# Two-layer hybrid backbone: separate PSUM banks and a ScalarE bias for the modulation values, and the first queries on VectorE

## The chip, the cores and the metric

The kernel runs on one core of one Trainium2 chip. The metric is the device time of one execution in microseconds (us). Engines are named as in the profile: PE is TensorE with PEld its weight loads, DVE is VectorE, ACT is ScalarE, POOL is GpSimd, and SP is SyncE, which issues most of the DMA.

## The reference, cut to what matters

The model has two layers over 512 latent tokens and 256 context tokens of width 1024. Each layer takes six modulation vectors from a conditioning vector by one large product with `ada_w` and a bias; the first and the fourth shift, the second and the fifth scale as `1 + scale`, and the third and sixth weigh the residuals. Layer 0 mixes by a gated convolution of 31 taps beside an mLSTM, layer 1 by latent attention, and each layer ends in a feed-forward part with a short convolution.

```python
def _modulate(x, shift, scale):
    return _rms(x) * (1 + scale) + shift
...
def _conformer_mlstm_mixer(h_lat, h_ctx, w_in, gate_bias, conv_w, conv_b, ln_g, ln_b,
                           head_gain, w_out, with_ctx_out):
    lat = _ab_project(h_lat, w_in, gate_bias)      # a, g, q, k, v, o and the gates
    ctx = _ab_project(h_ctx, w_in, gate_bias)
...
        a, g, _, _, _, o, _, _ = p
        u = _dwconv(a * jax.nn.sigmoid(g), conv_w, conv_b)        # 31 taps
        u = jax.nn.silu(_layer_norm(u, ln_g, ln_b))
...
def _mla_mixer(...):
    def queries(cq, rotate):
        q = (_rms(cq) * q_norm) @ w_uq
        q = _rms(q.reshape(*q.shape[:2], MLA_HEADS, MLA_QK)) * q_gain
        return _rope_tail(q, cos, sin) if rotate else q
...
    for layer in range(DEPTH):
...
        mod_l = jnp.split((jax.nn.silu(c) @ ada_w[layer] + ada_b[layer])[:, None, :], 6, axis=-1)
        mod_c = jnp.split(jax.nn.silu(c_ctx) @ ada_w[layer] + ada_b[layer], 6, axis=-1)
        h_lat = _modulate(xl, mod_l[0], mod_l[1])
        h_ctx = _modulate(xc, mod_c[0], mod_c[1])
...
        xl = xl + mod_l[2] * y_lat
        xl = xl + mod_l[5] * _conv_ffn(_modulate(xl, mod_l[3], mod_l[4]), ffn_w_in[layer],
                                       ffn_conv_w[layer], ffn_conv_b[layer], ffn_w_out[layer])
```

## The kernel before

All work is written for one stream of tokens, 768 columns wide (512 latent, 256 context), with channels on the 128 partitions. Products in float32 are split in a high and a low part (`wh`, `wl` for weights, `hh`, `hl` for activations) and three products of these are summed, so each block of weights costs one ScalarE copy (`wh`), one subtraction on VectorE or POOL (`wl`) and three matmuls. Tiles, semaphores and the order on each engine come from the tile framework: each engine works through its own instructions in order, and a write to a buffer waits for the buffer's last readers.

**Modulation values of layer 0.** Each of the six vectors is made in two halves of 512 columns. A unit is one half of one vector: `pada` is the product of the conditioning vectors with a block of `ada_w` (16 matmuls, `ada_mm`), `arow` its copy to SBUF by ScalarE (`ada_rows`), `pac` the sum over the four row groups, transposed to columns by four matmuls (`ada_cols`), and `mods` the sum with the bias `adab` (`ada_bias`), on VectorE. For the vectors that scale, a second operation adds 1, by way of the tile `amod`. Vectors 1 and 0 come first (`ada_first`). The six units of vectors 2, 3 and 4 come from the generator `ada_pe`, which is advanced while the values V of the mLSTM are projected (`vproj`). Per step it loads a unit's weights (`wa`, two loads of 1 MB by SP), finishes the unit before the last (`pac`), and multiplies the last (`pada`). Vector 5, and all of layer 1, is summed on VectorE instead (`ada_gemv`, `ada_sum`).

**Stages of `mixer0`, in the order of PE.** The first conv tile (`pa` and `pg` are the two halves of the gated unit), the gates `pgt`, the second tile, the projections `pqk`, the third and fourth tile, V (`pv`, in four parts of weights), then the column sums `pcol`, the gate `po` and the mLSTM (`pu` to `pn`). Of each conv tile, ScalarE evacuates `up` and `sg`, VectorE multiplies them (`up<-sg,up`), ScalarE writes the first tap into `acc`, and VectorE adds the other 30 taps one by one (`acc<-up,par,acc`, 128x783). The taps are a background list from which each step of the projections takes a few; VectorE works on them long after PE has passed on.

**PSUM.** The eight banks are one pool per stage, by tags. Until the mLSTM, the pool `WIDE` has one tag S with four buffers of two banks each. `psum` takes from S; `psum1`, for results of one bank (`pada`, `pac`), takes from a tag T where there is one, and from S otherwise.

```python
    def psum1(self, s="ps"):
        return self.pt("T" if "T" in self.ptags else "S", s)
```

**Queries of layer 1.** `prep_q` projects four heads' queries (`puq`), scales them by the reciprocal root of their mean square (`rq`) and rotates them. The first group is called from `mixer1` with POOL as the engine for the scaling and the rotation (one operation of 128x1536 and eight smaller ones); the others are called from `attention`. PE then turns queries and keys (`ptr<-ident,qt`, `ptr<-ident,kt`) for the scores.

## Time and profile before

| | us |
|---|---|
| median of 3 runs (lowest, highest) | 1783.36 (1781.83, 1787.54) |
| the profiled execution | 1782.59 |
| its span, first to last instruction | 1780.8 |
| PE busy | 1679.1 (94%) |
| VectorE busy | 1130.3 (63%) |
| ScalarE busy | 679.2 (38%) |
| POOL busy | 246.0 (14%) |
| mean granted clock of TensorE, of 1 | 0.960 |

Times in the rows below are counted from the start of the span. A row of the timeline gives start, duration (of all its instructions where it stands for several), and in brackets how long the engine was idle before and what ended that. Matmuls of one accumulation overlap, so the distance between two starts is the better measure of what one costs.

### The profile page before, as it was taken

The numbers are of one execution on the slowest core, as the hardware profiler recorded it, in microseconds if no ns is written. First come the engines' busy times: TensorE is split into PE (matmuls) and PEld (weight loads), VectorE is DVE, ScalarE is ACT, GpSimd is POOL, SyncE is SP. The second block draws the span as 40 slices with busy tenths as digits, with TensorE's granted clock in tenths as the row PEclk, the third lists the DMA queues.
The fourth block names the chain that finished last, engine by engine and source line by source line (L and its number), as shares of the span: only waits on it lengthen the run. The fifth ranks groups of instructions, "written<-read, shape, count | busy, mean of one in ns | idle before, by whom it ended". The sixth has DMA issues, their size and how long they took to land.

```text
span 1780.8 us, 24171 instructions
## 1 busy us (share of the span) xinstructions
PE 1679.1 (94%) x9436; PEld 1519.1 (85%) x9436; DVE 1130.3 (63%) x1743; ACT 679.2 (38%) x1364; POOL 246.0 (14%) x331
## 2 busy tenths in 40 slices
PE   6998698769999999999999998999999799999999
PEld 3998476659899999999999878999988788888887
DVE  3799964745876555474334487777788854444544
ACT  4421042542331221212222346777876442332232
POOL 2342132425100000000000111223140200000000
PEclk8999799779999999999999999999999899999999
DMA  9621442233253345262221332001110133333332
GB/s 311 216 61 42 135 143 83 61 118 100 74 159 106 108 142 166 84 200 67 64 60 49 97 96 61 32 13 36 44 35 25 36 95 97 101 98 95 95 95 83
DMA packets 194747, 168.43 MB, mean 95 GB/s; under 512 B 8552, under 2 KB 168214, under 8 KB 194632
## 3 DMA queue, kind: packets, MB, share of 16 engines
q1 hardware_dynamic: 191936, 163.30, 29.8%
q0 software_dynamic: 1280, 3.35, 0.8%
q8 instruction: 75, 1.23, 0.3%
q10 hardware_dynamic: 1416, 0.21, 0.1%
q14 instruction: 40, 0.33, 0.1%
HBM read 161.55 MB, written 5.29 MB: 94 GB/s over the span
## 4 chain that ended last, share of the span: by engine, by line
PE 81%; DVE 10%; DMA 3%; ACT 3%; issue 1%; POOL 1%; SPq 0%; ACTq 0%; DVEq 0%; POOLq 0%
PE pfo L110 17%; PE pfg L110 16%; PE pfv L110 16%; DVE acc L593 6%; PE psc L110 4%; PE pab L110 3%; PE ppv L110 2%; PE pt L1409 2%; PE po L110 2%; PE pf L110 2%; PE pmo L110 2%; PE puq L110 2%; PE pukv L110 2%; PE pv L110 1%; PE pn L110 1%
## 5 line engine op out<-in xcount | busy, mean ns | idle before, releaser
L113 ACT ACTIVATE wh<-wr 128x1024 fp32r<-128x1024 f32 (+3 forms) x205 | 204.4, 999 | 625.0 <-PE pfo L110 215.5
L167 DVE TENSOR_TENSOR wl<-wr,wh 128x1024 fp32r<-128x1024 f32 (+3 forms) x171 | 195.8, 1147 | 194.4 <-ACT wh L113 190.5
L110 PE MATMUL pfo<-hh,wh 128*128 128x384 f32 (+2 forms) x528 | 166.8, 355 | 0.0
L110 PE MATMUL pfo<-hl,wh 128*128 128x384 f32 (+2 forms) x528 | 166.6, 355 | 0.0
L110 PE MATMUL pfo<-hh,wl 128*128 128x384 f32 (+2 forms) x528 | 166.2, 354 | 0.0
L110 PE MATMUL pfg<-fh,wh 128*128 128x384 f32 (+1 forms) x504 | 152.0, 355 | 0.0
L110 PE MATMUL pfg<-fl,wh 128*128 128x384 f32 (+1 forms) x504 | 151.6, 354 | 0.0
L110 PE MATMUL pfg<-fh,wl 128*128 128x384 f32 (+1 forms) x504 | 151.2, 354 | 0.0
L110 PE MATMUL pfv<-fh,wl 128*128 128x384 f32 (+1 forms) x504 | 150.8, 353 | 0.0
L110 PE MATMUL pfv<-fl,wh 128*128 128x384 f32 (+1 forms) x504 | 150.8, 353 | 0.0
L110 PE MATMUL pfv<-fh,wh 128*128 128x384 f32 (+1 forms) x504 | 150.7, 353 | 0.0
L119 DVE SCALAR_TENSOR_TENSOR xr<-pfo,mods,xr 128x512 f32<-128x512 f32 (+1 forms) x128 | 83.7, 665 | 104.4 <-PE pfo L110 103.8
L593 DVE SCALAR_TENSOR_TENSOR acc<-up,par,acc 128x783 f32<-128x783 f32 x120 | 146.9, 1249 | 4.4 <-ACT acc L113 2.3
L167 POOL TENSOR_TENSOR wl<-wr,wh 128x1024 fp32r<-128x1024 f32 (+1 forms) x34 | 85.3, 2512 | 296.9 <-ACT wh L113 280.2
L253 POOL TENSOR_TENSOR ss<-ss,sq 128x256 f32<-128x256 f32 (+1 forms) x31 | 32.1, 1044 | 573.5 <-ACT sq L113 572.6
L119 DVE SCALAR_TENSOR_TENSOR ga<-gr,cc,ga 128x1024 f32<-128x1024 f32 (+1 forms) x84 | 96.0, 1161 | 22.6 <-DMA gr<-in_ada_w_dram 22.3
L110 PEld LDWEIGHTS pfo<-hl,wh 128*128 128x128 f32 x528 | 98.1, 189 | 8.9 <-issue 0.2
L110 PEld LDWEIGHTS pfo<-hh,wh 128*128 128x128 f32 x528 | 97.9, 189 | 9.0 <-ACT hh L113 0.4
L110 PEld LDWEIGHTS pfo<-hh,wl 128*128 128x128 f32 x528 | 97.9, 189 | 8.7
L116 DVE TENSOR_TENSOR ft<-ft,pfv 128x768 f32<-128x768 f32 (+1 forms) x42 | 34.4, 820 | 109.9 <-PE pfv L110 109.9
L110 PEld LDWEIGHTS pfg<-fh,wh 128*128 128x128 f32 x504 | 92.8, 189 | 6.5
L110 PEld LDWEIGHTS pfg<-fl,wh 128*128 128x128 f32 x504 | 92.8, 189 | 6.4
(418 smaller groups left out, 3711.0 us busy)
## 6 DMA issues: line engine op xcount, KB each, us to landing
wr<-in_ffn_w_in_dram SPq DMA_DIRECT2D x88, 512.0 KB, 4.0
gr<-in_ada_w_dram SPq DMA_DIRECT2D x48, 512.0 KB, 4.5
wa<-in_ada_w_dram SPq DMA_DIRECT2D x20, 1024.0 KB, 8.1
wr<-in_ffn_w_out_dram SPq DMA_DIRECT2D x32, 512.0 KB, 3.5
wr<-in_ab_w_in_dram SPq DMA_DIRECT2D x20, 512.0 KB, 5.2
wr<-in_ffn_w_out_dram SPq DMA_DIRECT2D x24, 384.0 KB, 3.3
gr<-in_ada_w_dram SPq DMA_DIRECT2D x16, 256.0 KB, 2.7
wr<-in_mla_w_out_dram SPq DMA_DIRECT2D x8, 512.0 KB, 3.4
```

The lines of the kernel that those rows point to most:

```text
L110: self.nc.tensor.matmul(out, lhsT=lhsT, rhs=rhs, start=start, stop=stop)
L113: self.nc.scalar.activation(out, in_, func, **kw)
L116: self.nc.vector.tensor_tensor(out, a, b, op=op)
L119: self.nc.vector.scalar_tensor_tensor(out, a, s, b, op0=op0, op1=op1, **kw)
L167: self.lo_eng.tensor_tensor(lo[:, :n], raw[:, :n], hi[:, :n].bitcast(F32), op=ALU.subtract)
L253: eng.tensor_tensor(self.ss[:, s:e], self.ss[:, s:e], sq[:, s:e], op=ALU.add)
L593: nc.vector.scalar_tensor_tensor(acc[:, :CONVO], up[:, k:k + CONVO], self.convw[:, 4 * k + ct:4 * k + ct + 1], acc[:, :CONVO], op0=ALU.mul ...
L1409: nc.tensor.transpose(pt[:, o:o + P], pe[:, (j + jj) * P:(j + jj + 1) * P], self.ident)
```

## The change

Four edits. Until the mLSTM, the eight banks are three double banks (tag S) and two single ones (tag T, for `pada`, `pac` and the other results of one bank). For the six units of `ada_pe`, ScalarE adds the bias to `pac`, by one activation of 128x2 for each of the four columns of a half. The 1 of the scaling vectors is added to the bias itself, once per layer (`one_plus`). And the first group of queries is scaled and rotated by VectorE.

```diff
--- before.py
+++ after.py
@@ -69,6 +69,7 @@
 AFR = 4
 RUNS = (0, 0, 4, 4, 1, 1, 5, 5, 2, 2, 6, 3, 3, 7)
 WIDE = {"S": (2, 4)}
+FRONT = {"S": (2, 3), "T": (1, 2)}
 MLSTM = {"S": (2, 2), "M": (2, 2)}
 
 VW = P + 1
@@ -285,12 +286,12 @@
         self.act(rows, ps[:, :512])
         return rows
 
-    def ada_cols(self, rows, layer, mod, k1):
+    def ada_cols(self, rows, layer, mod, k1, on_act=True):
 
         p2 = self.psum1("pac")
         for k in range(4):
             self.mm(p2[:, 2 * k:2 * k + 2], rows[:, k * P:(k + 1) * P], self.selq, True, True)
-        self.ada_bias(p2, layer, mod, k1, 4)
+        self.ada_bias(p2, layer, mod, k1, 4, on_act)
 
     def ada_first(self, h, pool):
 
@@ -303,7 +304,7 @@
                 self.nc.sync.dma_start(raw, w[k * P:(k + 4) * P, c0:c0 + 512].rearrange("(k p) c -> p k c", p=P))
                 for kk in range(4):
                     self.ada_mm(ps, raw[:, kk], k + kk)
-            self.ada_cols(self.ada_rows(ps), 0, mod, 4 * h)
+            self.ada_cols(self.ada_rows(ps), 0, mod, 4 * h, False)
 
     def ada_pe(self, layer, mods, pool):
 
@@ -365,17 +366,21 @@
                 self.mm(p2[:, 2 * k:2 * k + 2], a[:, k * P:(k + 1) * P], self.selv[:, v, :], v == 0, v == len(accs) - 1)
         self.ada_bias(p2, layer, mod, k1, n)
 
-    def ada_bias(self, p2, layer, mod, k1, n):
+    def ada_bias(self, p2, layer, mod, k1, n, on_act=False):
         o = self.mods[layer][:, mod, k1:k1 + n, :]
         k0 = mod * KD + k1
-        b = self.adab[layer][:, k0:k0 + n].unsqueeze(2).to_broadcast([P, n, 2])
+        b = self.adab[layer][:, k0:k0 + n]
         pv = p2[:, :2 * n].rearrange("p (k v) -> p k v", v=2)
-        if mod in (1, 4):
-            tmp = self.small.tile([P, KD, 2], F32, tag="amod", name=self.name("amod"))[:, :n]
-            self.tt(tmp, pv, b, ALU.add)
-            self.nc.vector.tensor_scalar(o, tmp, 1.0, None, op0=ALU.add)
+        if on_act:
+            for k in range(n):
+                self.act(o[:, k], pv[:, k], AF.Identity, bias=b[:, k:k + 1])
         else:
-            self.tt(o, pv, b, ALU.add)
+            self.tt(o, pv, b.unsqueeze(2).to_broadcast([P, n, 2]), ALU.add)
+
+    def one_plus(self, ab):
+
+        x = ab[:, :48].rearrange("p (m k) -> p m k", k=KD)[:, 1::3]
+        self.nc.vector.tensor_scalar(x, x, 1.0, None, op0=ALU.add)
 
     def setup(self):
         nc, tc, d, ctx = self.nc, self.tc, self.d, self.ctx
@@ -430,6 +435,7 @@
         nc.vector.tensor_copy(self.cc32[:, :, :2], self.cc)
         ab = ctile([P, 48], "adab0")
         nc.vector.tensor_copy(ab, pa[:, 16:64])
+        self.one_plus(ab)
         self.adab.append(ab)
 
     def cols_load(self, q, st, parts):
@@ -481,6 +487,7 @@
         nc.vector.tensor_scalar(self.convw[:, :4 * CW], self.convw[:, :4 * CW], 0.5, None, op0=ALU.mult)
         nc.vector.tensor_scalar(v[:, 0:12], v[:, 0:12], 0.5, None, op0=ALU.mult)
         nc.vector.tensor_scalar(v2[:, 88:89], v2[:, 88:89], float(QK) ** -0.5, None, op0=ALU.mult)
+        self.one_plus(ab)
         self.adab.append(ab)
         self.lng, self.lnb, self.hgain, self.qnorm, self.kvnorm = (
             v[:, 0:4], v[:, 4:8], v[:, 8:12], v[:, 12:16], v[:, 16:18])
@@ -1225,7 +1232,7 @@
                     nc.vector.tensor_scalar(kvt[t][:, :256], kvt[t][:, :256], rk[:, t:t + 1], None, op0=ALU.mult)
                 qt0 = self.query_tile(ap)
                 for _ in self.prep_q(0, qt0, cqs, tb, wuq, lambda: tmp("sq")[:, :4 * QK].rearrange("p (h c) -> p h c", c=QK),
-                                     [xs[k][:, LAT:T] for k in (2, 3)], nc.gpsimd):
+                                     [xs[k][:, LAT:T] for k in (2, 3)], nc.vector):
                     pass
                 for k in range(2):
                     ps = self.psum("pkvT")
@@ -1530,7 +1537,7 @@
     def run(self):
         nc, tc = self.nc, self.tc
         pes = ExitStack()
-        self.psum_pool(pes, WIDE)
+        self.psum_pool(pes, FRONT)
         self.setup()
         xs = self.mixer0(pes)
         self.dump("x_mix0", xs)
```

Where the instructions move. On PE, in the V projection, the first `pac` (`pac_1520`, now `pac_1518`) was followed by nine matmuls of the second part of V and then by the second `pada`; these are the rows of the kernel before:

```order
L110 MATMUL pac_1520<-selq,arow_1463 128x2 x3
L110 MATMUL pv_165_1443<-wh_1538,hh_412 128x512
L110 MATMUL pv_165_1443<-wl_1539,hh_412 128x512 [waits Pool_49]
L110 MATMUL pv_165_1443<-wh_1538,hl_413 128x512
L110 MATMUL pv_165_1443<-wh_1538,hh_414 128x512
L110 MATMUL pv_165_1443<-wl_1539,hh_414 128x512
L110 MATMUL pv_165_1443<-wh_1538,hl_415 128x512
L110 MATMUL pv_165_1443<-wh_1538,hh_412 128x512
L110 MATMUL pv_165_1443<-wl_1539,hh_412 128x512
L110 MATMUL pv_165_1443<-wh_1538,hl_413 128x512
L110 MATMUL pada_1526<-wa_1450,cc_107 32x512 [waits DMAHW1_49,DVE_49]
L110 MATMUL pada_1526<-wa_1450,cc_107 32x512 x3
```

With the change the same place reads:

```order
L111 MATMUL pac_1518<-selq,arow_1461 128x2 [waits Activation_49]
L111 MATMUL pac_1518<-selq,arow_1461 128x2 x3
L111 MATMUL pada_1527<-wa_1448,cc_107 32x512 [waits DMAHW1_49,PE_49]
L111 MATMUL pada_1527<-wa_1448,cc_107 32x512 x3
L111 MATMUL pada_1527<-wa_1449,cc_107 32x512 [waits DMAHW2_49]
L111 MATMUL pada_1527<-wa_1449,cc_107 32x512 x3
L111 MATMUL pv_163_1441<-wh_1539,hh_409 128x512
L111 MATMUL pv_163_1441<-wl_1540,hh_409 128x512 [waits Pool_49]
```

The second `pada` has moved ahead of the second part of V, and its wait for VectorE (`DVE_49`) has become one for PE's own earlier use of the bank. The `pac` that follows comes behind all 36 matmuls of that part.

On ScalarE, from the `arow` of the first unit to that of the second, before (`acc_1426` is the first tap of the fourth conv tile):

```order
L113 ACTIVATE arow_1463<-pada_1454 128x512 [waits PE_49]
L113 ACTIVATE acc_1426<-up_1418,par 128x783 [waits DVE_49,Pool_49]
L113 ACTIVATE wh_1680<-wr_1679 128x1024 [waits DMAHW1_49,PE_49,Activation_49]
L113 ACTIVATE arow_1535<-pada_1526 128x512 [waits PE_49,Activation_49]
L113 ACTIVATE wh_1831<-wr_1830 128x1024 [waits DMAHW2_49,PE_49,Pool_49]
```

And with the change:

```order
L114 ACTIVATE arow_1461<-pada_1452 128x512 [waits PE_49]
L114 ACTIVATE acc_1424<-up_1416,par 128x783 [waits DVE_49,Pool_49]
L114 ACTIVATE wh_1687<-wr_1686 128x1024 [waits DMAHW1_49,PE_49,Activation_49]
L114 ACTIVATE mods_111<-pac_1518,adab_194 128x2 [waits PE_49]
L114 ACTIVATE mods_111<-pac_1518,adab_194 128x2 x3
L114 ACTIVATE arow_1536<-pada_1527 128x512 [waits PE_49,Activation_49]
L114 ACTIVATE wh_1843<-wr_1842 128x1024 [waits DMAHW2_49,PE_49,Pool_49]
```

Four additions of the bias (`mods`) have come in ahead of the second `arow`, and all of them stand behind `acc`, which waits for VectorE.

On VectorE, in the preparation of the attention, from the last step of `rq` on; `v` are evacuations of the values, `wl` low parts of weights, and what follows leads to the scale `rk` of the keys. Before:

```order
L119 SCALAR_TENSOR_TENSOR rz_8602<-rz_8602,ra_8601 128x16
L119 SCALAR_TENSOR_TENSOR rq_8600<-rz_8602,rq_8600 128x16
L116 TENSOR_TENSOR v_8675<-pukv_8677,v_8675 128x4x64
L167 TENSOR_TENSOR wl_8915<-wr_8913,wh_8914 128x768
L116 TENSOR_TENSOR v_8675<-pukv_8698,v_8675 128x4x64
L116 TENSOR_TENSOR ssk_8676<-ssk_8676,ssr 128x12
L199 TENSOR_SCALAR ra_8742<-ssk_8676 128x12
L116 TENSOR_TENSOR v_8675<-pukv_8719,v_8675 128x4x64
```

And with the change, up to the last but two of the nine operations that POOL had:

```order
L120 SCALAR_TENSOR_TENSOR rz_8610<-rz_8610,ra_8609 128x16
L120 SCALAR_TENSOR_TENSOR rq_8608<-rz_8610,rq_8608 128x16
L1308 TENSOR_TENSOR qt_8526<-qt_8526,rq_8608 128x1536
L117 TENSOR_TENSOR v_8683<-pukv_8685,v_8683 128x4x64
L1316 TENSOR_TENSOR xr_2911<-qt_8526,sq 128x128
L168 TENSOR_TENSOR wl_8923<-wr_8921,wh_8922 128x768
L1316 TENSOR_TENSOR xr_2911<-qt_8526,sq 128x128
L1316 TENSOR_TENSOR xr_2913<-qt_8526,sq 128x128
L1318 TENSOR_TENSOR qt_8526<-qt_8526,cq 128x8x32
L1316 TENSOR_TENSOR xr_2913<-qt_8526,sq 128x128
L1319 TENSOR_TENSOR qt_8526<-qt_8526,xr_2911 128x8x32
L1318 TENSOR_TENSOR qt_8526<-qt_8526,cq 128x8x32
```

The scaling of `qt` and the rotation (`xr`, `qt`) now stand between `rq` and the sums `ssk` of the keys; on POOL the same nine are gone.

## Rows read from the trace of the kernel before

**Rows 1.** The page, part 4: share of each engine in the chain.
```profile
PE 81%; DVE 10%; DMA 3%; ACT 3%; issue 1%; POOL 1%; SPq 0%; ACTq 0%; DVEq 0%; POOLq 0%
```

**Rows 2.** Windows: stretch, its length; busy us (instructions) by engine; granted clock; DMA share, GB/s.
```profile
180.00:230.00 50.00, 32.34 (x166) 21.56 (x165) 49.11 (x49) 5.65 (x7) 10.82 (x3) 0.83 0.46 149
```

**Rows 3.** Timeline of PE, 160 to 290 us: start, duration, instructions, [idle before <-releaser].
```profile
174.62 0.63 PE L110 MATMUL pv<-wl,hh 128*128 128x512 f32 x1
...
179.31 0.60 PE L110 MATMUL pv<-wh,hh 128*128 128x512 f32 x1
...
182.30 0.95 PE L110 MATMUL pac<-selq,arow 128*128 128x2 f32 x8
...
203.11 3.64 PE L110 MATMUL pada<-wa,cc 128*32 128x512 f32 x16 [17.66 <-DVE mods L116]
...
207.18 0.39 PE L110 MATMUL pv<-wl,hh 128*128 128x512 f32 x1
...
213.22 0.95 PE L110 MATMUL pac<-selq,arow 128*128 128x2 f32 x8
...
220.72 1.92 PE L110 MATMUL pada<-wa,cc 128*32 128x512 f32 x16
```

**Rows 4.** Timeline of DVE, 188 to 280 us.
```profile
191.24 0.69 DVE L119 SCALAR_TENSOR_TENSOR up<-sg,up 128x512 f32<-128x512 f32 x1
...
202.90 0.15 DVE L116 TENSOR_TENSOR mods<-pac,adab 128x8 f32<-128x8 f32 x1
...
276.06 0.42 DVE L116 TENSOR_TENSOR kw<-pu,wcol 128x256 f32<-128x256 f32 x1 [24.67 <-PE pu L958]
```

**Rows 5.** Timeline of ACT, 168 to 250 us.
```profile
174.81 0.81 ACT L113 ACTIVATE sg<-pg 128x768 f32<-128x768 f32 x1
...
193.30 1.04 ACT L113 ACTIVATE acc<-up,par 128x783 f32<-128x783 f32 x1 [17.19 <-DVE up L119]
194.25 1.04 ACT L113 ACTIVATE wh<-wr 128x1024 fp32r<-128x1024 f32 x1
206.88 0.60 ACT L113 ACTIVATE arow<-pada 128x512 f32<-128x512 f32 x1 [11.59 <-PE pada L110]
...
245.90 0.27 ACT L113 ACTIVATE ccol<-pcol 128x24 f32<-128x24 f32 x2 [1.82 <-PE pcol L881]
...
248.43 1.88 ACT L113 ACTIVATE ex<-ex,ccol 128x128 f32<-128x128 f32 x6
```

**Rows 6.** Timeline of PE, 219 to 262 us.
```profile
235.84 0.95 PE L110 MATMUL pac<-selq,arow 128*128 128x2 f32 x8
...
239.41 1.05 PE L110 MATMUL pac<-selq,arow 128*128 128x2 f32 x8 [0.78 <-ACT arow L113]
...
246.56 1.01 PE L110 MATMUL po<-hh,wh 128*128 128x384 f32 x2 [0.69 <-ACT em L113]
```

**Rows 7.** Timeline of PE, 17 to 50 us.
```profile
27.74 1.87 PE L110 MATMUL pac<-selq,arow 128*128 128x2 f32 x8 [0.78 <-ACT arow L113]
...
30.21 2.92 PE L110 MATMUL pb<-rx,runs 6*128 6x128 f32 x12 [0.37 <-DVE rx L560]
```

**Rows 8.** Timeline of POOL, 1095 to 1116 us.
```profile
1102.39 2.76 POOL L1301 TENSOR_TENSOR qt<-qt,rq 128x1536 f32<-128x1536 f32 x1 [65.86 <-DVE rq L119]
```

**Rows 9.** Timeline of DVE, 1095 to 1116 us.
```profile
1102.05 0.18 DVE L119 SCALAR_TENSOR_TENSOR rq<-rz,rq 128x16 f32<-128x16 f32 x1
...
1104.44 1.52 DVE L167 TENSOR_TENSOR wl<-wr,wh 128x768 fp32r<-128x768 f32 x1 [0.79 <-ACT wh L113]
...
1108.52 0.65 DVE L119 SCALAR_TENSOR_TENSOR rz<-rz,ra 128x12 f32<-128x12 f32 x1
...
1112.22 0.96 DVE L1362 TENSOR_TENSOR kt<-kt,rk 128x768 f32<-128x768 f32 x1
1113.09 0.55 DVE L1363 TENSOR_TENSOR kt<-krr,rk 128x384 f32<-128x384 f32 x1
```

**Rows 10.** The page, part 6: DMA issues, KB each, us to landing.
```profile
wa<-in_ada_w_dram SPq DMA_DIRECT2D x20, 1024.0 KB, 8.1
```

## The prediction

> **What bounds the kernel now.** I read the chain that ended last first: PE has 81% of it and VectorE 10% [rows 1], so a change is worth what it gives PE where PE stands still. The windows show where that is: from 180 to 230 us PE is busy 32.34 of 50 us at a granted clock of 0.83, while VectorE is busy 49.11 [rows 2]. The timeline of PE names the wait: at 203.11 the modulation product `pada` starts after 17.66 us of idle that VectorE's `mods` ended [rows 3]. The timeline of VectorE shows this releaser: an addition of 0.15 us at 202.90, in order behind the taps of the convolution [rows 4]. It waited only because `pada` needed the bank that this addition reads. The reader is to see that PE waits for a tiny instruction in a long queue, and that VectorE itself then has 24.67 us to spare before its first `kw` [rows 4]: its taps end at 276.06 - 24.67 = 251.4.
>
> **The change part by part.**
>
> *Banks and the bias on ScalarE.* `pada` no longer waits for VectorE, but ScalarE becomes the next in line. Behind the `arow` of the first unit, its queue holds `acc` of the fourth conv tile, which waits for VectorE's `up` until 193.30, then `wh` at 194.25 (ending about 195.3) [rows 5]; behind these stand the four new additions and the next `arow`. The new order lets PE run the first `pac`, the second `pada` and all 36 matmuls of the second part of V, and then the second `pac` waits for that `arow`. So the wait is not removed: it becomes later and shorter.
>
> How far PE gets: the first `pac` starts at 182.30 and a `pada` takes 1.9 [rows 3]. From the `pac` at 235.84 over a `pada` and a wait of 0.78 to the next `pac` it is 3.57 us [rows 6], so a `pac` takes 3.57 - 0.78 - 1.9 = 0.89. A matmul of V takes (213.22 - 207.18)/26 = 0.232 us, so 36 take 8.35. PE stops at 182.30 + 0.89 + 1.9 + 8.35 = 193.4.
>
> When it goes on: no row shows an addition of 128x2 with a bias held in a tile. Bounds: the two `ccol` of 128x24 without one take 0.27 together, so 0.19 and then about 0.09 a step, 0.46 for four; the six `ex` of 128x128, which have such a bias, take 1.88, 0.31 each, of which at least 0.1 is for the 126 columns more, leaving about 0.2, so at most 4 x 0.23 = 0.93 [rows 5]. I take 0.9, for `ex` shares the bias operand. With 0.6 for `arow` [rows 5], PE goes on at 195.3 + 0.9 + 0.6 = 196.8, after an idle of 3.4 us.
>
> A rule of the Trainium skill speaks against this part: "ScalarE: Activation LUTs", section "What ACT_TABLE_LOAD costs", says that an activation pays a fixed start, longer with a bias from a tile (about 280 ns, consecutive ones overlapping by 93 ns), so that one operation split into four pays it four times. By the page, an estimate, the four would take about 0.85 us, and the total would come out 0.1 us lower than by the row that I use; no row here shows the operation itself.
>
> Before, PE reached the second `pac` at 213.22 [rows 3]: 16.4 us later. But after an idle the clock is lower: in the matmuls of V from 174.62 on, which follow a wait, eleven took (179.31 - 174.62)/11 = 0.43 each instead of 0.23 [rows 3], 2.3 us in all with a twelfth. I charge the new idle with the same 2.3 (bounds 0 and 2.3), and save nothing for the old one, since what that cost lay ahead of 213.22.
>
> From there to `po` the new order has five `pac` (4.45), four `pada` (7.6), two parts of V with 36 matmuls each (16.7), the 18 transposes `pcol`, one wait of 0.78 for `arow`, and 0.95 for the last four additions, for which `po` waits. `pcol` follows from the old end: 239.41 + 0.89 + 1.9 + 0.78 + 0.89 = 243.87, and to 246.56, less the wait of 0.69, 2.0 us are left [rows 6]. Sum 32.5; before it was 246.56 - 213.22 = 33.3, with one wait of 0.78 more, which `pcol` now covers. So `po` starts at 196.8 + 32.5 + 2.3 = 231.6 instead of 246.56: **15.0 us gained**.
>
> Is it carried on? VectorE's taps end at 251.4 less some 1 to 2 us for the additions taken out; `kw` is now wanted at 276.06 - 15.0 = 261.1. Some ten us are left, so VectorE does not become the bound. The loads of the last units: a `wa` lands 8.1 us after its issue [rows 10]; the last pair takes the buffers of the fourth `pada`, which by the steps above ends about 213, so it lands at 221 and is wanted at 227. That covers 6 us of delay in SP's queue.
>
> *Three double banks instead of four.* PE now waits for evacuations that a fourth bank covered. The narrowest place is the fourth conv tile: its `sg` is evacuated by 174.81 + 0.81 = 175.6 and used by VectorE at 191.24 [rows 4, 5]: 15.6 us of cover. I take 0 (bounds 0 and 1).
>
> *The start.* With `pr` and `pb` no longer in line behind a `pac` at 27.74, which waited 0.78 for `arow` and takes 0.89 [rows 7], they come about 1.7 us before the old 30.21, and everything that follows from `pb` (normalised tiles, first weights, first taps) with them. Bounds 0 and 2; I take **1.5 us gained**, and since VectorE's taps, which begin from there, fill it (49.11 of 50 us in the window above), it moves ScalarE's `acc` at 193.30, and so all of the above, by the same amount.
>
> *Queries on VectorE.* POOL's nine operations go; the first took 2.76 us for 128x1536 [rows 8]. On VectorE: from 384 columns in 0.55 and 768 in 0.96 [rows 9], 1536 take 0.96 + 2 x 0.41 = 1.8; four of 128x128 at about 0.2 and four of 256 at 0.34: 3.9 us added between 1102.2 and `kt`. Against that, while POOL ran, a `wl` of 128x768 took 1.52 instead of 0.96 and a small operation 0.65 (1108.52) instead of 0.18 (1102.05) [rows 9]. Some eight small ones stand there; at half of the 0.47 of that row, for not all are as slow, they and the `wl` give back 2.4 us. VectorE also waited 0.79 for ScalarE in front of that `wl` [rows 9] and about as much once more ahead of it; the new operations fill these 1.6 us. A further 0.7 comes off the copies of `v` and the later `wl`. So 3.9 added stand against 4.7 given back: `kt`, which ends at 1113.09 + 0.55 = 1113.6 [rows 9], and PE's transposes behind it, come **0.8 us earlier**. Bounds: 2 gained, or 4 lost if nothing is hidden.
>
> *The added 1 folded into the bias*: two short VectorE operations in the set-up, of some 0.2 us like the small ones above. In the feed-forward part the additions taken out have PE-bound work around them. I take 0 for both.
>
> Sum: 1782.59 (the profiled execution: its span of 1780.8 and 1.8 around it; the median of the runs is 0.8 above) - 15.0 - 1.5 - 0.8 = 1765.3. **I predict 1765 us.**
>
> **The rivals.**
>
> *A. The wait disappears altogether.* If `acc` comes as PE ends the part, neither the 3.4 us of idle nor the 2.3 of slow clock remain: 1765 - 5.7 = 1759. For it: nothing but that `up` could come earlier with the start. Against it: ScalarE works in order and `up` of the fourth tile depends on VectorE's taps, which moves by 1.5 only. 8%.
>
> *B. Part of it is handed back.* Each later `pac` waits a little longer for ScalarE, with its four additions ahead of the next `arow`, or the last `wa` pairs land late, and the clock stays low through the short waits: 3 to 8 us, so 1768 to 1773. For it: short waits of 0.78 and 0.69 are there already [rows 6]. Against it: in each of the two long parts 8 us of matmuls lie between a `pada` and its `pac`. 17%.
>
> *C. The change does not do what it says.* PE still waits for VectorE, only by way of ScalarE's `acc`, and the later gain is lost in the attention's preparation: with `po` at 240, the start at 0 and 4 lost behind `kt`, 1782.6 - 6.5 + 4 = 1780. For it: that chain of waits is real. Against it: `acc` comes at 193.30, ten us ahead of 202.90. 4%.
>
> *D. Slower.* With three double banks, PE in the gated unit waits for evacuations that stand in ScalarE's queue behind an `acc` waiting for VectorE, so `up` is late and the taps stop. The place is the fourth conv tile, ahead of 191.24. Up to 15.6 us it is covered; to pass the time before, the delay must reach 15.6 + 17.3 = 33 us. A hold of 40 us would give 1765 + 40 - 15.6 = 1789. For it: one bank less of four. Against it: the evacuations that free these banks stand ahead of the `acc` in ScalarE's order. 3%.
>
> **How the numbers follow.** My forecast has 68% and its own range is 1761 to 1768 (slow clock 0 to 2.3, start 0 to 2, additions 0.46 to 0.93, queries -2 to +4). With A below and most of B above, 1758 to 1771 leaves out less than 2 in 10. A difference under 0.3% (5 us) is about what this measurement can't tell from none. The forecast, A and B are faster: 93%; C and what else could cancel it give 4% within, D 3% slower.
>
> **What would show it right or wrong.** Right: the wait of `pada` for VectorE is gone; PE idles some 3 us before 196 (195 with the start's gain) and names ScalarE's `arow`; matmuls of V behind it take 0.43 for some five us; `po` starts near 230; VectorE waits for `pu` about 9 us instead of 24.67; in the attention's preparation no POOL work beside VectorE's, small VectorE operations of 0.17, `kt` a little sooner relative to `rq`. Wrong: a wait of PE for `wa` or `mods` between 200 and 230, a gap in the taps before 193, or a longer stretch from `rq` to `kt`.

## The result and the profile after

| | before | changed |
|---|---|---|
| median of the runs, us (lowest, highest) | 1785.45 (1781.83, 1788.24), 4 runs | 1767.49 (1762.60, 1771.46), 4 runs |
| ratio to before, 95% interval | | 0.9899 (0.9863 to 0.9936) |
| the profiled execution; its span, us | 1782.59; 1780.8 | 1762.60; 1760.4 |

The changed kernel is faster by 1.0%, some 18 us between the medians; 1765 was predicted. Its own executions differ among themselves: the two shorter ones have a mean granted clock of 0.966, the two longer ones 0.961 and 0.960; of the runs below, one of `change_wl`, of 2378 us at a granted clock of 0.646, is left out.

The timeline of PE in V, in the kernel after, answers to [rows 3]:
```profile
184.99 0.95 PE L111 MATMUL pac<-selq,arow 128*128 128x2 f32 x8
185.87 1.92 PE L111 MATMUL pada<-wa,cc 128*32 128x512 f32 x16
...
195.81 0.39 PE L111 MATMUL pv<-wh,hl 128*128 128x512 f32 x1
199.01 1.25 PE L111 MATMUL pac<-selq,arow 128*128 128x2 f32 x8 [2.81 <-ACT arow L114]
200.19 3.36 PE L111 MATMUL pada<-wa,cc 128*32 128x512 f32 x16
203.48 0.50 PE L111 MATMUL pv<-wh,hh 128*128 128x512 f32 x1
...
232.34 0.62 PE L111 MATMUL po<-hh,wh 128*128 128x384 f32 x2 [0.81 <-ACT mods L114]
```
The second `pada` follows its `pac` at once; the 17.66 us of idle in front of it are gone. In their place stand 2.81 us in front of the second `pac`, for ScalarE's `arow`. Behind it `pac` and `pada` run at a lower clock (3.36 instead of 1.92), and the matmuls of V from 203.48 are at full pace again. `po` comes at 232.34 instead of 246.56.

The windows of the kernel after (the stretch of [rows 2], then 11 us of which the last 1.8 are in the idle, and 4 us behind it; busy us of PE, PEld, DVE, ACT and POOL, granted clock, DMA share, GB/s):
```profile
180.00:230.00 50.00, 46.88 (x263) 32.51 (x262) 49.57 (x46) 14.81 (x48) 24.15 (x4) 0.94 0.62 209
...
187.00:198.00 11.00, 9.20 (x44) 6.68 (x36) 10.75 (x13) 2.12 (x4) 0.00 (x0) 1.00 0.70 235
199.00:203.00 4.00, 3.99 (x24) 1.75 (x24) 4.00 (x2) 1.62 (x5) 4.00 (x2) 0.59 0.18 40
```
PE now fills 46.88 of the 50 us instead of 32.34. The clock of 0.59 of its 2.4 GHz, nearly the level of 1.2 GHz, lies wholly behind the idle.

The timeline of ACT around the same place answers to [rows 5]:
```profile
195.88 1.04 ACT L114 ACTIVATE acc<-up,par 128x783 f32<-128x783 f32 x1 [17.20 <-DVE up L120]
196.83 1.04 ACT L114 ACTIVATE wh<-wr 128x1024 fp32r<-128x1024 f32 x1
197.78 0.69 ACT L114 ACTIVATE mods<-pac,adab 128x2 f32<-128x2 f32 x4
198.35 0.60 ACT L114 ACTIVATE arow<-pada 128x512 f32<-128x512 f32 x1
```
This is the chain that PE waits for, in ScalarE's order: `acc` waits 17.20 us for VectorE's `up`, and the four additions and `arow` stand behind it. The four take 0.69 us.

The timeline of DVE answers to [rows 4]:
```profile
193.82 0.69 DVE L120 SCALAR_TENSOR_TENSOR up<-sg,up 128x512 f32<-128x512 f32 x1
...
228.33 3.12 DVE L600 SCALAR_TENSOR_TENSOR acc<-up,par,acc 128x783 f32<-128x783 f32 x1
231.38 3.14 DVE L117 TENSOR_TENSOR s<-s,acc 128x783 f32<-128x783 f32 x1
...
255.61 0.97 DVE L117 TENSOR_TENSOR s<-s,acc 128x783 f32<-128x783 f32 x1
260.91 0.42 DVE L117 TENSOR_TENSOR kw<-pu,wcol 128x256 f32<-128x256 f32 x1 [4.33 <-PE pu L965]
```
The first `kw` is 15.15 us earlier (276.06 before), and VectorE has 4.33 us to spare in front of it instead of 24.67.

The timeline of PE at the start, from the profiled execution after, answers to [rows 7]:
```profile
20.21 1.92 PE L111 MATMUL pada<-wa,cc 128*32 128x512 f32 x16
...
25.48 2.80 PE L111 MATMUL pb<-rx,runs 6*128 6x128 f32 x12 [0.37 <-DVE rx L567]
...
30.92 1.87 PE L111 MATMUL pac<-selq,arow 128*128 128x2 f32 x8 [0.78 <-ACT arow L114]
32.72 3.47 PE L111 MATMUL pada<-wa,cc 128*32 128x512 f32 x16
38.99 1.61 PE L111 MATMUL pac<-selq,arow 128*128 128x2 f32 x8 [2.80 <-ACT arow L114]
...
44.95 1.87 PE L111 MATMUL pac<-selq,arow 128*128 128x2 f32 x8 [0.78 <-ACT arow L114]
46.68 0.99 PE L111 MATMUL pa<-hh,wh 128*128 128x384 f32 x2
```
`pb` is 4.7 us earlier, but the `pac` that was ahead of it is 3.2 later (30.92, before 27.74). The third `pada` is still a little earlier than before, and then PE waits longer for `arow`; the same two rows before:
```profile
33.07 3.54 PE L110 MATMUL pada<-wa,cc 128*32 128x512 f32 x16
...
37.40 1.05 PE L110 MATMUL pac<-selq,arow 128*128 128x2 f32 x8 [0.79 <-ACT arow L113]
```
The timeline of ACT in the kernel after shows where that `arow` stands:
```profile
37.73 0.72 ACT L114 ACTIVATE hh<-u,mods 128x512 fp32r<-128x512 f32 x1 [0.15 <-DVE u L120]
38.36 0.58 ACT L114 ACTIVATE arow<-pada 128x512 f32<-128x512 f32 x1
```

The timeline of DVE in the attention's preparation answers to [rows 9]:
```profile
1080.94 1.02 DVE L120 SCALAR_TENSOR_TENSOR kvl<-pkvT,par,kvh 128x768 fp32r<-128x768 f32 x1
...
1084.75 1.76 DVE L1308 TENSOR_TENSOR qt<-qt,rq 128x1536 f32<-128x1536 f32 x1
...
1086.96 0.96 DVE L168 TENSOR_TENSOR wl<-wr,wh 128x768 fp32r<-128x768 f32 x1
...
1091.26 0.17 DVE L120 SCALAR_TENSOR_TENSOR rz<-rz,ra 128x12 f32<-128x12 f32 x1
...
1093.59 0.96 DVE L1369 TENSOR_TENSOR kt<-kt,rk 128x768 f32<-128x768 f32 x1
```
The 128x1536 takes 1.76 on VectorE, where POOL took 2.76 [rows 8]; the `wl` takes 0.96 and the small operations 0.17, with no wait in front of the `wl`.

Where the 20.4 us between the two spans went: 15.15 are there at the first `kw`. From the first `kvl` to `kt` the changed kernel takes 12.65 instead of 13.78, and from `kt` to the first `psc` 3.08 instead of 3.67: 1.7 together. Most of the remaining 3.5 lies in stretches that the change does not touch: 2.1 from `kw` to the first feed-forward part, and 1.3 from `psc` to the second. The repeat below gives these back.

### The profile page after: what moved, and what is told of

Same layout as the page of the kernel before. It is cut to its first block, busy times and chain, and to the rows that moved or that the text cites. A ratio compares the mean times of both kernels' runs of the same rounds, so it can differ in the third digit from the quotient of the medians.

```text
span 1760.4 us, 24187 instructions
## 1 busy us (share of the span) xinstructions
PE 1674.3 (95%) x9436; PEld 1513.3 (86%) x9436; DVE 1133.5 (64%) x1742; ACT 683.6 (39%) x1388; POOL 254.7 (14%) x322
## 4 chain that ended last, share of the span: by engine, by line
PE 84%; DVE 10%; ACT 3%; issue 1%; DMA 1%; POOL 1%; SPq 0%; ACTq 0%; POOLq 0%; DVEq 0%
PE pfo L111 17%; PE pfg L111 17%; PE pfv L111 16%; DVE acc L600 4%; PE psc L111 4%; PE pab L111 4%; PE ppv L111 2%; PE pt L1416 2%; PE po L111 2%; PE pv L111 2%; PE pf L111 2%; PE pmo L111 2%; PE puq L111 2%; PE pukv L111 2%; PE pac L111 2%
## 5 line engine op out<-in xcount | busy, mean ns | idle before, releaser
L600 DVE SCALAR_TENSOR_TENSOR acc<-up,par,acc 128x783 f32<-128x783 f32 x120 | 151.2, 1285 | 4.5 <-ACT acc L114 2.3
L168 POOL TENSOR_TENSOR wl<-wr,wh 128x1024 fp32r<-128x1024 f32 (+1 forms) x34 | 100.9, 2975 | 265.5 <-ACT wh L114 248.8
```

Source lines behind the costliest of these rows:

```text
L168: self.lo_eng.tensor_tensor(lo[:, :n], raw[:, :n], hi[:, :n].bitcast(F32), op=ALU.subtract)
L600: nc.vector.scalar_tensor_tensor(acc[:, :CONVO], up[:, k:k + CONVO], self.convw[:, 4 * k + ct:4 * k + ct + 1], acc[:, :CONVO], op0=ALU.mul ...
```

## The experiments

Each kernel's runs alternated with runs of the kernel before on the same chip, whose median was 1784.4 to 1784.9; ratios are against it.

**The changed kernel once more**, without an edit.

> The changed kernel again, unaltered, so that the other runs have it on the same chip. Theory (the gain is PE's earlier return in the V projection, some 14 to 17 us, less about 2 lost at the start): the second pac starts near 199 after about 3 us of idle for ScalarE's arow, po starts at 232 +- 1, the median is 1762 to 1768. Rival (a part of the 20 us between the two profiled executions is a difference between executions): po near 232 all the same, but the median 1768 to 1772.

Measured: median 1769.95 (1763.74 to 1771.06, 5 runs), ratio 0.9911 (0.9896 to 0.9925). The profiled execution was one of the longer ones, at a granted clock of 0.960. PE waits 2.94 us for `arow` at 198.06, `po` comes at 234.74, `kw` at 263.89 behind 9.22 us of spare time. The two stretches that the change does not touch take 189.5 and 306.9 us, where before took 189.2 and 306.7 and the first profile 187.1 and 305.4. So the 3.4 us there are differences between executions. Together with the 4.33 and 9.22 us of slack, the reader sees how far one profile carries: some 3 us in a landmark, some 5 in a wait.

**The banks alone**: additions on VectorE as before, queries on POOL, the pool FRONT and the folded 1 kept.
```diff
-    def ada_cols(self, rows, layer, mod, k1, on_act=True):
+    def ada_cols(self, rows, layer, mod, k1, on_act=False):
...
-                                     [xs[k][:, LAT:T] for k in (2, 3)], nc.vector):
+                                     [xs[k][:, LAT:T] for k in (2, 3)], nc.gpsimd):
```

> Only the banks and the folded 1: the sums stay on VectorE, the first queries on POOL. Theory (banks and bias each free PE by half): the second pada starts at once, but the second pac reuses the bank of the first, which VectorE reads only behind its taps, so PE idles 7 to 9 us there, names DVE mods, goes on near 204.5, and po starts at 237 to 240; median some 6 us above the changed kernel. Rival (the banks alone do it): idle under 3.5 us, po within 1 us of the changed kernel, the time within 2 us of it.

Measured: 1782.74, ratio 0.9992 (0.9980 to 1.0004). The timeline of PE in this kernel:
```profile
206.21 1.84 PE L111 MATMUL pac<-selq,arow 128*128 128x2 f32 x8 [12.10 <-DVE mods L117]
...
240.81 1.84 PE L111 MATMUL pac<-selq,arow 128*128 128x2 f32 x8 [6.21 <-DVE mods L117]
...
249.13 1.01 PE L111 MATMUL po<-hh,wh 128*128 128x384 f32 x2 [0.26 <-DVE mods L117]
```
The wait moves from `pada` to the next `pac`, still for VectorE. It is a third shorter than the 17.66 us of before, and what that wins is paid for by a second one at the end of V. `po` is at 249.13, not earlier than before.

**The bias alone**: the additions on ScalarE and the folded 1, the pool WIDE as before, queries on POOL.
```diff
-                                     [xs[k][:, LAT:T] for k in (2, 3)], nc.vector):
+                                     [xs[k][:, LAT:T] for k in (2, 3)], nc.gpsimd):
...
-        self.psum_pool(pes, FRONT)
+        self.psum_pool(pes, WIDE)
```

> Only the bias on ScalarE and the folded 1: four double banks as before, the first queries on POOL. Theory: the second pada still needs the bank of the first pac and waits for ScalarE's additions behind acc, until about 196 (10 us of idle instead of 17.7), with 27 matmuls of its part still to come; po starts near 239, 7 us sooner than before; the start is as before, with the first pada near 17.3 and the first pa near 44.4; median 7 us under the kernel before. Rival (the bias alone does it): po near 232.

Measured: 1785.94, ratio 1.0006 (0.9998 to 1.0015). The timeline of PE:
```profile
198.15 3.64 PE L111 MATMUL pada<-wa,cc 128*32 128x512 f32 x16 [11.94 <-ACT mods L114]
...
234.96 1.94 PE L111 MATMUL pada<-wa,cc 128*32 128x512 f32 x8 [2.68 <-DMA wa<-in_ada_w_dram]
...
251.30 1.01 PE L111 MATMUL po<-hh,wh 128*128 128x384 f32 x2 [0.69 <-ACT em L114]
```
`pada` still waits for the bank, now for ScalarE behind its `acc`: 5 us earlier than the 203.11 of before, though the first tap is 2.3 us later in this profile (73.49, before 71.20). At the end of V the loads `wa` come late, and nothing is left at `po`. The timeline of POOL, then the waits of SP's queue (the loads that SP issues) from 180 to 245 us (total, times, longest), name the cause:
```profile
210.36 17.82 POOL L168 TENSOR_TENSOR wl<-wr,wh 128x1024 fp32r<-128x1024 f32 x1 [9.78 <-ACT wh L114]
```
```profile
SPq L166 <- POOL wl L168: 48.8, 5, 25.9
```
SP waits for this `wl` before it may load the next raw weights `wr` into their buffer, at 228.21, and issues the `wa` behind that, from 228.68 on.

**The queries alone**, in the kernel before.
```diff
-                                     [xs[k][:, LAT:T] for k in (2, 3)], nc.gpsimd):
+                                     [xs[k][:, LAT:T] for k in (2, 3)], nc.vector):
```

> The kernel before with one edit: the first four heads' queries scaled and rotated by VectorE. Theory (VectorE's own work gives back what POOL's cost it): from the last kvl to kt 12.7 us instead of 13.8, and to the first psc 15.7 to 16.4 instead of 17.4, nothing else changed; median 1 to 2 us under the kernel before, less than the measurement can tell. Rival (nothing hidden): kvl to kt 16 us or more, the time 2 to 4 us longer.

Measured: 1784.66, ratio 0.9996 (0.9987 to 1.0005). In the trace, `kvl` to `kt` takes 12.66 and `kt` to `psc` 3.67: 1.1 us less than before, all of it ahead of `kt`. That is under what the times can tell from nothing, and they show nothing. The start of this kernel is that of the kernel before, and its first tap comes at 73.26, before at 71.20: two profiles of one start differ by 2 us.

**The start with the old banks**: WIDE until the tokens are loaded, FRONT from there on.
```diff
                 xs, rstd = self.load_x(hpa, sl)
                 par = self.params_load(sl)
+                pes.close()
+                pes = ExitStack()
+                self.psum_pool(pes, FRONT)
...
-        self.psum_pool(pes, FRONT)
+        self.psum_pool(pes, WIDE)
```

> The changed kernel, but with four double banks until x is loaded and transposed, and the new banks from there. Theory (three double banks hold the transposes of x, which delays the first pada from 17.3 to 20.2, the loads behind it by 3 us, and so the first weights): the first pada is back at 17.3 +- 0.5, the first pa at 42 to 44.5 instead of 46.7, and with it the taps and po 2 to 4 us sooner; median 2 to 4 us under the changed kernel. Rival (the late first pa comes from the order of pb and hh or from the loads, not from the banks): pa stays at 46 to 47.

Measured: 1767.62, ratio 0.9912 (0.9898 to 0.9927), no change from the repeat. The timeline of PE at the start of this kernel:
```profile
19.17 1.92 PE L111 MATMUL pada<-wa,cc 128*32 128x512 f32 x16 [0.90 <-ACT x L114]
...
44.58 0.61 PE L111 MATMUL pa<-hh,wh 128*128 128x384 f32 x2
...
47.03 1.01 PE L111 MATMUL pa<-hh,wl 128*128 128x384 f32 x2 [1.50 <-POOL wl L168]
```
The first half of the theory held. The transposes `px` end at 18.27 here; in the profiles with four double banks at this place (before, `queries_only`, `bias_only` and this one) they end at 17.3 to 18.3, in the nine with three at 18.8 to 20.3. The first `pada` is two us later than the 17.34 of before all the same, for it waits 0.90 more for ScalarE's last copy `x` of them. The second half fell: the first `pa` is as early as before, but then waits for a `wl`, and the first tap comes at 72.91, no sooner than in the changed kernel.

**The first tap of the fourth tile on VectorE**, so that ScalarE's additions and `arow` stand behind no `acc` that waits.
```diff
+                w0, b0 = self.convw[:, ct:ct + 1], self.convw[:, 124 + ct:125 + ct]
+                if ct == 3:
+                    nc.vector.tensor_scalar(acc[:, :CONVO], up[:, 0:CONVO], w0, b0, op0=ALU.mult, op1=ALU.add)
+                else:
+                    self.act(acc[:, :CONVO], up[:, 0:CONVO], AF.Identity, scale=w0, bias=b0)
```

> The changed kernel, with the first tap of the fourth conv tile on VectorE (one operation of 128x783 with two scalars, some 0.6 us there), so that ScalarE has nothing in its queue that waits for VectorE between 178 and 196. Theory (what holds PE at the second pac is the acc of that tile, ahead of the additions and arow): the idle of 2.8 to 2.9 us before the second pac is gone, and so is the low clock behind it (1.5 us or more), po starts 4 to 5 us sooner relative to the first tap; VectorE's taps end 0.6 later, so that its idle before kw falls to between 0 and 5 us; median 3 to 5 us under the changed kernel (some 1765). Rival (four additions ahead of each arow hold PE by themselves, or the clock stays low in any case): 2 us of idle or more remain there, the time stays within 1.5 us.

Measured: 1765.30, ratio 0.9891 (0.9877 to 0.9905). The wait in front of the second `pac` is gone and `po` starts at 224.68, 7.7 us earlier than in the changed kernel (5.9, counted from the first tap). But inside `po` PE waits 4.56 us for ScalarE's `so` at 247.75, and the first `kw` is at 260.63, as in the changed kernel.

**The first taps of the third and fourth tile on VectorE**: the same with `ct >= 2`.

> As tap3_dve, and the first tap of the third tile on VectorE too. ScalarE then evacuates up as soon as PE has it, instead of behind an acc that waits until 173. Theory (VectorE is the next bound): the 7 us of idle in the first part of V are gone as well, and PE comes to po some 13 us sooner, near 219, but VectorE's taps end no sooner (near 257), so PE now waits for VectorE at kw, 8 us or more, with the clock low behind it; kw near 257.5, the median only 1 to 4 us under the changed kernel, no better than tap3_dve. Rival (PE is still the bound): kw follows PE, the median 10 to 13 us under the changed kernel.

Measured: 1763.89, ratio 0.9887 (0.9871 to 0.9902). Now the wait of 7.0 for `up` in the first part of V is gone too, and `po` starts at 218.59. The timeline of PE there:
```profile
218.59 1.01 PE L111 MATMUL po<-hh,wh 128*128 128x384 f32 x2 [0.81 <-ACT mods L114]
...
246.13 1.01 PE L111 MATMUL po<-hh,wh 128*128 128x384 f32 x2 [8.49 <-ACT so L114]
```
The timeline of POOL shows what is behind it:
```profile
208.67 22.55 POOL L168 TENSOR_TENSOR wl<-wr,wh 128x1024 fp32r<-128x1024 f32 x1 [8.53 <-ACT wh L114]
235.69 0.91 POOL L1014 TENSOR_SCALAR_AFFINE_SELECT ex<-ex 128x512 f32<-128x512 f32 x1 [4.47 <-DMA ex<-ad]
```
And the timeline of ACT links the two:
```profile
236.63 2.60 ACT L114 ACTIVATE ex<-ex,ccol 128x128 f32<-128x128 f32 x8 [15.49 <-POOL ex L1014]
...
245.29 0.79 ACT L114 ACTIVATE so<-po 128x768 f32<-128x768 f32 x1
```
Read backwards: `po` waits for ScalarE's `so`; `so` stands behind ScalarE's `ex`, which waits 15.49 us for POOL's `ex`; and POOL was busy for 22.55 us with one `wl`, after which the load of `ex` was still on its way. 13.7 us gained at `po` are 2.4 at `kw`. I had held VectorE to be the next limit; it is not yet (2.48 us to spare).

**The same with gate `po`'s low weights on VectorE instead of POOL** (`tap23_wl`), and that edit alone on the changed kernel (`change_wl`).
```diff
+                    self.lo_eng = nc.vector
                     w = self.weights(win, 0, KD, 2048 + m * P, P)
+                    self.lo_eng = nc.gpsimd
```

> As tap23_dve, and the low parts of the four weights of the gate po on VectorE instead of POOL. Theory (PE's new wait of 8.5 us for so is the POOL wl of 22.55 us, which the unbroken taps of VectorE hold up, with SP's loads and the ex behind it): no POOL instruction over 6 us from 195 on, the wait of po for so is gone or under 2 us, the taps end near 255 in spite of four operations of 1.15 more, for they are stretched less; kw at 250 to 256 instead of 258.5, the median 3 to 8 us under tap23_dve (some 1757 to 1761). Rival (so waits for the load of ex itself): the wait for so stays at 6 us or more, the time within 1.5 us of tap23_dve.

Measured: 1768.34, ratio 0.9909 (0.9894 to 0.9923): no better. The long `wl` of POOL is gone, but its `ex` starts no earlier (240.71), so it was the load of `ex` that set it as well. A new wait stands in V:
```profile
221.79 1.93 PE L111 MATMUL pada<-wa,cc 128*32 128x512 f32 x8 [14.12 <-DMA wa<-in_ada_w_dram]
```
The waits of SP's queue in this kernel, from 180 to 240 us (total, times, longest), name the cause:
```profile
SPq L166 <- DVE wl L168: 46.9, 3, 28.9
```
The loads of the raw weights `wr` wait for the buffers that VectorE's late `wl` still reads, and `wa` stands behind them in SP's order.

> The changed kernel with the low parts of the four weights of the gate po on VectorE. Theory (in the changed kernel the long wl on POOL, 17.47 us, is still just covered: no engine waits for it): PE's waits from 160 to 260 and the start of po stay as they are, kw within 1.5 us, the median within 2 us of the changed kernel. Rival (it is what PE's time from po to kw hangs on already): kw 3 us sooner or more, the median 3 us lower.

Measured: median 1765.91 of three runs, ratio 0.9894 (0.9874 to 0.9914); `po` at 232.63, `kw` at 261.85. In the changed kernel POOL's long `wl` is covered, and taking it away brings nothing.

**Gate `po`'s weights later in the order** (`wl_late`): as `tap23_wl`, with a priority that puts `wa` ahead of them in SP's queue.
```diff
-                    w = self.weights(win, 0, KD, 2048 + m * P, P)
+                    w = self.weights(win, 0, KD, 2048 + m * P, P, 150)
```

> As tap23_wl, with the loads of the gate's weights at a lower priority, so that SP issues the last modulation weights (wa) ahead of the third of them. Theory (the 14.1 us for wa in tap23_wl are SP's queue, held by a wr that waits for a wl on VectorE): that wait is under 3 us, po starts at 218 to 224, the taps end near 248; the loads of ex still stand behind two wr in SP's queue, so PE may wait for so by up to 8 us; kw at 250 to 257, the median 1756 to 1762, under tap23_dve (1764) by 2 us or more. Rival (the loads themselves are late, whatever the order): 8 us or more for wa remain.

Measured: 1771.86, ratio 0.9922 (0.9910 to 0.9935), slower than `tap23_dve`. The wait for `wa` is gone and `po` is at 218.89, but its matmuls with `wl` wait 4.87 for that, and at 253.05 it waits 9.09 for `so`: POOL's `ex` starts at 242.84 only, 64.35 us after its work before, for the load `ex`, which stands in SP's queue behind weights.

**And the loads of the first two `ex` and `ib` from POOL's queue** (`wl_late_ex`).
```diff
-                nc.sync.dma_start(ex[i].rearrange("p h n -> p (h n)"),
+                (nc.gpsimd if s < 2 else nc.sync).dma_start(ex[i].rearrange("p h n -> p (h n)"),
...
-                nc.sync.dma_start(ib[64 * b:64 * b + 64],
+                (nc.gpsimd if s < 2 else nc.sync).dma_start(ib[64 * b:64 * b + 64],
```

> As wl_late, and the first two token blocks' loads of ex and ib from POOL's queue instead of SP's. Theory (after the taps, the wl and wa, what is late is ex, by SP's queue): the wait of po for so is gone or under 2 us, kw follows PE or the end of the taps, whichever is later, at 248 to 254, the median 1753 to 1759. Rival (PE is held elsewhere by then, or loads from POOL's queue come later): no better than wl_late.

Measured: 1760.38 (1757.86 to 1762.44), ratio 0.9860 (0.9847 to 0.9874), the fastest kernel of the study, some 7 us under the changed one. The timeline of PE, then that of DVE:
```profile
225.43 1.01 PE L111 MATMUL po<-hh,wl 128*128 128x384 f32 x2 [6.25 <-DVE wl L168]
```
```profile
255.97 0.42 DVE L117 TENSOR_TENSOR kw<-pu,wcol 128x256 f32<-128x256 f32 x1 [1.33 <-PE pu L970]
```
No wait for `so` or `wa` is left. What remains are 8.4 us for `wl` in two waits, and VectorE has only 1.33 us to spare: here it is nearly the limit. Whether the loads from POOL's queue would do as much on `tap23_dve`, without the two edits between, was not tried.

## Why the prediction was right, and where its terms were off

The gain of 17.3 us was predicted from the profiled execution; the medians lie 18.0 apart in the first comparison and 14.7 in the repeat. A single term of 1 or 2 us can't be read from that total; the landmarks below show each.

**The main step held.** PE's wait for `mods` ends up at the second `pac`, later and shorter, for an `arow` behind ScalarE's `acc`: 3.4 us were predicted, 2.81 and 2.94 measured. For `po` the prediction started from a first tap at the time of before. Counted from the first tap (71.20 before, 73.58 and 72.67 in the two profiles after), the way to `po` shrank from 175.36 (175.34 in `queries_only`) to 158.76 and 162.07: 16.6 and 13.3 us, around the 15.0 predicted. The clock makes the difference between the two. Behind the idle it costs 1.7 us in the first profile (1.25 and 3.36 instead of 0.95 and 1.92) and about 3 in the repeat, where `pac` and `pada` take 1.51 and 3.64 and four matmuls of V behind them 0.43 each; 2.3 was charged. Just ahead of `po` the repeat loses 1.8 more to it (a `pada` of 2.90, a `pac` of 1.87), which the prediction did not have.

**Neither half alone shows in the time, and the two together give the 1%.** 0.9992 and 1.0006 against 0.99, with the queries at 0.9996. The bank made `pada` wait for `mods`, and VectorE made `mods` late. Undoing one of the two cut the wait from 17.66 to some 12 us, and each time the rest came back at the end of V in another way. With only its own bank, the additions still stand in VectorE's queue, and a second `pac` waits 6.21 for them. With only ScalarE, PE was 6.8 us ahead at the fourth `pac`, counted from the first tap (157.85 behind it, before 164.64), and lost this to the late `wa`, behind POOL's `wl` of 17.82 us; from 235 to 252 its granted clock was 0.50, before 0.80. The same `wl` took 4.92 before (last section). What the bias alone would be worth with these loads in time was not tried. The prediction worked out the two together only.

**The four additions with a bias from a tile** take 0.69 to 0.74 us, inside the bounds of 0.46 to 0.93 (the upper one, by its own working of 0.21 each, is 0.85); 0.9 was taken. By the rule of the Trainium skill named in the prediction ("ScalarE: Activation LUTs", section "What ACT_TABLE_LOAD costs") they would, as an estimate, have taken about 0.85. The trace agrees that the fixed part is paid four times (each takes 0.24 to 0.27 us for two columns and starts 0.14 behind the last), and comes out 0.11 to 0.16 us below.

**The start is the step that failed: 1.5 us gained were predicted, and none are seen.** The first tap comes at 73.58 and 72.67 in the two profiles after, at 71.20 in that of before and at 73.26 in `queries_only`, with the same start as before; over all profiles it lies at 71.2 to 73.5 with the old order and at 70.9 to 73.6 with the new. So a loss isn't shown either. I let everything follow from `pb`. `pb` did come 4.7 us earlier, and though PE enters its row of `pada` and `pac` 2 to 3 us later, behind the longer `px` (first `pada` at 20.21 and 19.21; 17.34 before), it is 0.4 and 1.2 us ahead at the third `pada` (32.72 and 31.83; 33.07 before). There it loses the lead, by the same tie as in V. The first activations `hh` also need the `mods` of the second `pac`, which now stands behind `pb`; so they come only 0.9 us earlier (33.02, before 33.96), and now five of them and two more, which wait for VectorE's `u`, stand in ScalarE's queue ahead of the next `arow`. The next `pac` waits 2.80 and 2.98 us for that `arow`, before 0.79, and from the third `pada` to the first `pa` it is 14.0 and 14.2 us instead of 11.3 (12.5 in `queries_only`).

**VectorE had less to spare than some ten us**: 4.33 and 9.22 measured. Of the missing part up to 2.4 us is the first tap, later in these profiles than in that of before; and the taps do not become shorter with the additions gone: from the first tap to the last sum, 180.2 us before, are 183.0 and 182.0 after. The rows at 228.33 and 231.38 above, 3.12 and 3.14 us for operations of about 1, show some of it: they lie beside POOL's `wl` (last section). It did not matter for the total.

**The queries** gave 1.1 us ahead of `kt`, in the changed kernel and when put into the kernel before (0.8 predicted); the other 0.6 behind `kt` are in the changed kernel alone and not shown to be theirs. Each part is as worked out: 1.76 for the largest, `wl` back at 0.96, small ones at 0.17, the wait filled.

**Three double banks cost nothing** in the gated units, as taken: the stretch from the first tap to the fourth tile's `up` at 193.82 is 120.2 us in both profiles after, and 120.0 before, so the taps never stopped for an evacuation. What they cost is some two us at `px`, where the prediction did not look.

**Of the rivals**, C and D did not occur. A, the wait vanishing, was made by hand (`tap3_dve`): PE has the time at `po` and has lost it again at `kw`. At 1759 A counted too much: behind this wait stands the next. B, part of it handed back by later `pac` or by `wa`, did not occur in the changed kernel but for the 1.8 us of low clock in the repeat; late `wa` did with the bias alone and in `tap23_wl`.

## What to carry to other kernels

When a matmul waits for a tiny instruction in a long queue, look for both ties, the buffer that connects them and the queue that makes the instruction late: here undoing either tie alone cut the wait by a third only, and the rest came back further on. Then follow the work moved through the queue it joins, for it waits behind what stands there, and ask what holds up the stage that now starts earlier; 13.7 us more at `po` were worth 2.4 at `kw`, and 4.9 once two further queues were rearranged. And a stage that "follows from" one early input follows from its latest one: at the start, another input of the same instruction decided.

## What the runs showed of the hardware

The same POOL subtraction of 128x1024 took about 3 us or 16 to 24 (15.89 in the repeat, 23.88 in `tap3_dve`), with the same work of VectorE beside it. The timeline of POOL in the changed kernel:
```profile
198.00 6.00 POOL L168 TENSOR_TENSOR wl<-wr,wh 128x1024 fp32r<-128x1024 f32 x2 [16.70 <-issue]
```
```profile
213.15 17.47 POOL L168 TENSOR_TENSOR wl<-wr,wh 128x1024 fp32r<-128x1024 f32 x1 [9.15 <-ACT wh L114]
```
and that of DVE beside them:
```profile
198.66 6.17 DVE L600 SCALAR_TENSOR_TENSOR acc<-up,par,acc 128x783 f32<-128x783 f32 x2
...
210.43 17.08 DVE L600 SCALAR_TENSOR_TENSOR acc<-up,par,acc 128x783 f32<-128x783 f32 x18
```
Each of the two at 198 cost one tap of VectorE some 2 us (two taps took 6.17, where one takes 1.0). The one at 213.15 got nowhere while VectorE ran its taps at full pace; it ended at 230.62, inside the tap of 3.12 us at 228.33 (shown above), as if it had its turn only there, behind VectorE's first sum `s`. In `tap23_dve` the `wl` of 22.55 us ends at 231.22, again inside a slow tap right behind that sum. The Trainium skill, "SBUF — State Buffer", section "Who interferes with whom", says that a VectorE instruction with two SBUF inputs contends with a POOL instruction that reads SBUF, and that the port pair they share is an exclusive lock. These rows agree with the exclusion, but the loser waited here for some fifteen instructions in a row. What lets POOL in stays open: at 198 it came in between two taps of an unbroken row. In the kernel before, this `wl` took 4.92 us at 214.61, with an addition `mods` in VectorE's queue at 217.19 and a slow tap of 3.06 us right behind that. `bias_only` has the banks of before and takes these additions off VectorE: there the same `wl` takes 17.82 us and ends, like the others, in a slow tap right behind the sum `s` (225.84, of 3.18 us). So in the kernel before this addition was the gap, as far as one run without it shows.
